# The first normalization's shift and scale in two halves of the channels, and the first projection begun on the lower half

## The chip, the core and the metric

The program runs on one NeuronCore of a Trainium2 chip. Its time is the device time of one execution in microseconds, given as the median of several runs. A NeuronCore has a matrix engine (TensorE, PE in the rows; PEld is its weight load), a vector engine (VectorE, DVE), an activation engine (ScalarE, ACT), a general engine (GpSimd, POOL), and a queue that mostly issues transfers (SyncE, SP). Each works through its own list of instructions in order and waits for the others by semaphores.

## What is computed

Two layers of a hybrid model over 512 tokens of 1024 channels. What matters here is the head of a layer:

```python
mod_all = einsum('bd,lde->lbe', silu(c), ada_w) + ada_b      # 6 vectors of 1024 a layer
sh1, sc1, g1, sh2, sc2, g2 = split(mod_all[l], 6)
h = _rms_norm(x, norm_mix_g[l]) * (1.0 + sc1) + sh1
proj = h @ w_in[l]                                           # 1024 -> 2732 columns
...
x = x + g1 * (mix @ w_out[l])
h2 = _rms_norm(x, norm_ffn_g[l]) * (1.0 + sc2) + sh2
x = x + g2 * _moe(h2, ...)
```

Four mixers (sparse attention, pooling, a linear recurrence, dilated attention) stand between `proj` and `mix`. All is in float32: each large product is made of three passes (`mm3`, L597) over a high part and a low part of both operands, so a weight tile is split into `wh` (a copy on ACT, L550) and `wl` (a difference on DVE, L551) before PE uses it.

## The kernel before

Tokens lie in four tiles of 128 (`xt`), channels in eight blocks of 128, called `k` = 0 to 7. Names that the text uses:

- **x**: four loads of 512 KB (L514). ACT squares and sums each tile in two halves (`square`, L788), DVE turns the four sums into `rs` (`rsqrt`), and ACT and DVE scale the tiles by it (L856 to L860).
- **tp**: four PE transposes for each block `k` (L868). ACT copies the result into `hf` (L876).
- **ada**: the product of silu(c) with `ada_w`. A unit of the stream `ada_s` is a 512 KB tile of two channel blocks by 512 output columns. The vectors scale (v = 1) and shift (v = 0) of the first normalization have two halves of 512 columns each (`jj`), and a half takes four units, so 16 units in all. Each unit is read by two program matmuls (L659), each of which leaves two records in the trace. DVE adds the partial sums to the table `MT` (L662). Four small matmuls `mc` (L721) turn the table into columns, from which DVE makes `A1` = (1 + scale) times gain (L882) and `B1` = shift (L883).
- **hH, hL**: block by block, `hf` becomes `hf * A1 + B1` (even blocks on DVE L897, odd ones on ACT L895), then its high part `hH` (ACT L898) and its low part `hL` (DVE L900).
- **c0**: the first 512 columns of the projection, transposed (`cchunk`, L908). Weights come in four units `u` of two channel blocks each; for each unit four sums `c` get six matmuls (L598 to L600), so 96 in all, 24 a unit. Block `k` = 2u + i of `hH` and `hL` is needed by unit `u` only. `c1` and others follow.

Loads are issued by the SP queue in the order in which the program asks for them (`Stream.load`, L563). The order on the other engines is written out by a planner (`_Weaver`, L366): a main stream of work is interleaved with side streams, by a clock of its own that adds up estimated durations (`_Clock`, L211). A side stream gets its next piece once that clock of PE has passed the moment at which the piece should be ready. So a change in the first stage also moves that clock, and by it the place of side work later on.

Of the kernel before, what the change touches and what calls it, by code (L numbers as in the profile page):

```python
# [11 lines left out]
F32 = mybir.dt.float32  # L12
# [4 lines left out]
AF = mybir.ActivationFunctionType  # L17
OP = mybir.AluOpType
# [416 lines left out]
def fused(ctx: ExitStack, tc: tile.TileContext, A, out, dbg=None):  # L435
    nc = tc.nc
    V, SC, PE, GP, SY = nc.vector, nc.scalar, nc.tensor, nc.gpsimd, nc.sync
# [12 lines left out]
    W = _Weaver(K)  # L450

    def G(name, shape=(1024,), dt=F32):

        t_ = gp.tile([128] + list(shape), dt, name=name, tag="g")
        K.alloc("g", NG, t_)
        return t_

    def HG(name, shape=(512,), dt=F32):

        t_ = hp.tile([128] + list(shape), dt, name=name, tag="h")  # L460
        K.alloc("h", NH, t_)
        return t_
# [4 lines left out]
    def TI(name, w=64, dt=F32):  # L467
        return tip.tile([128, w], dt, name=name, tag="ti")

    def PA(name):  # L470
        t_ = pa.tile([128, 512], F32, name=name, tag="a")
        K.alloc("a", NPA, t_)
        return t_

    def PB(name):
        t_ = pb.tile([128, 512], F32, name=name, tag="b")
        K.alloc("b", 8 - NPA, t_)
        return t_
# [31 lines left out]
    def load_x(src, q=None):  # L510
        r = []
        for t in range(NT):
            x_ = G("x")
            (q or SY).dma_start(x_, src[t * 128:(t + 1) * 128])  # L514
            r.append(x_)
        return r


    def rsqrt(x_, out_, n):

        xh, t_ = TI("rq_xh", n), TI("rq_t", n)
        V.tensor_scalar(xh, x_, -0.5, None, op0=OP.mult)
        V.tensor_scalar(out_.bitcast(I32), x_.bitcast(I32), 1, 0x7fffffff,
                        op0=OP.logical_shift_right, op1=OP.bitwise_xor)
        V.tensor_scalar(out_, out_, 1.835e-20, None, op0=OP.mult)
        for _ in range(3):
            V.tensor_tensor(t_, out_, out_, op=OP.mult)
            V.tensor_tensor(t_, t_, xh, op=OP.mult)
            V.scalar_tensor_tensor(out_, t_, 1.5, out_, op0=OP.add, op1=OP.mult)
# [67 lines left out]
    def mm3(o, sh, sl, mh, ml, first, last):  # L597
        PE.matmul(o, lhsT=sh, rhs=mh, start=first, stop=False)  # L598
        PE.matmul(o, lhsT=sh, rhs=ml, start=False, stop=False)  # L599
        PE.matmul(o, lhsT=sl, rhs=mh, start=False, stop=last)  # L600
# [23 lines left out]
    zc = cst.tile([128, 8, 63], F32, name="zc")  # L624
# [8 lines left out]
    MT = cst.tile([128, 512], F32, name="mt")  # L633
    MF = {(l, v): _Flag() for l in range(L) for v in range(6)}

    def mod_rows(l):
        GP.memset(MT, 0.0)
        GP.dma_start(MT[0:12], A["ada_b"][l])
        if l + 1 < L:
            GP.dma_start(MT[12:16], A["ada_b"][l + 1, 0:4])  # L640


    ada_s = Stream([(A["ada_w"][l, 2 * v + jj, u], 512) for l, v in
                    [(0, v) for v in (1, 0, 2, 4, 3, 5)] + [(1, v) for v in (1, 0, 2, 4, 3, 5)]
                    for jj in range(2) for u in range(4)], 3, raw=True)

    def ada(l, vs, more=True):
        if more:
            ada_s.cap += 8 * len(vs)
        for l2, v in vs:  # L650
            for jj in range(2):
                j = 12 * (l2 - l) + 2 * v + jj
                ps = PB("ada")
                for u2 in range(2):
                    raws = [ada_s.get() for _ in range(2)]
                    yield
                    for i in range(4):
                        g, k = 32 * i, 4 * u2 + i
                        PE.matmul(ps[g:g + 32], lhsT=zc[:, k, 31 - j:63 - j], rhs=raws[i // 2][:, i % 2],  # L659
                                  start=u2 == 0, stop=u2 == 1)  # L660
                    if u2:
                        V.tensor_tensor(MT, MT, ps, op=OP.add)  # L662
                    MF[l2, v].done, MF[l2, v].ready = u2 == jj == 1, K.mark
                    yield
# [52 lines left out]
    def mcol(p_, j0, n):  # L717

        v_ = p_[:, 0:4 * n].rearrange("p (q j) -> p q j", q=4)
        for q in range(4):  # L720
            PE.matmul(v_[:, q], lhsT=MT[:, q * 128:(q + 1) * 128], rhs=C("sel")[:, j0:j0 + n], start=True, stop=True)  # L721
        return v_

    def qj(ap):

        return ap.rearrange("p (j q) -> p q j", j=2)
# [61 lines left out]
    def square(x_, ms):  # L788

        m2 = TI("m2", 2)  # L790
        for j in range(2):
            SC.activation(PB("jk"), x_[:, j * 512:(j + 1) * 512], AF.Square, accum_out=m2[:, j:j + 1])
        V.tensor_tensor(ms, m2[:, 0:1], m2[:, 1:2], op=OP.add)

    def rms(xt, n=NT):
        ms = TI("ms", n)
        for t in range(n):
            square(xt[t], ms[:, t:t + 1])
        V.tensor_scalar(ms, ms, 1.0 / D, EPS, op0=OP.mult, op1=OP.add)
        rs_ = TI("rs_", n)  # L800
        rsqrt(ms, rs_, n)
        return rs_
# [38 lines left out]
    def layer(l, xt, mixs, moes, nmixs):  # L841
        last = l + 1 == L
        P_ = pars.pop(l)
        col, pr, omm, hv = P_.col, P_.pr, P_.omm, P_.hv
# [8 lines left out]
        if l == 0:  # L853
            P_.scaled()
            rs = rms(xt)
            for t in range(NT):  # L856
                if t % 2:
                    V.tensor_scalar(xt[t], xt[t], rs[:, t:t + 1], None, op0=OP.mult)
                else:
                    SC.activation(xt[t], xt[t], AF.Copy, scale=rs[:, t:t + 1])  # L860
        hH = [G("hH", (2, 512), F32R) for _ in range(4)]
        hL = [G("hL", (2, 512), F32R) for _ in range(4)]
        hf = [G("hf", (2, 512)) for _ in range(4)] if l == 0 else None

        def transposed(k):
            tp = PB("tp")
            for t in range(NT):
                PE.transpose(tp[:, t * 128:(t + 1) * 128], xt[t][:, k * 128:(k + 1) * 128], ident)  # L868
            return tp

        if l == 0:
            mc = PA("mc")
            A1, B1 = TI("A1", 8), TI("B1", 8)
            for k in range(8):
                tp = transposed(k)
                SC.activation(hf[k // 2][:, k % 2], tp, AF.Copy)  # L876
            ada_s.cap = 16
            ada_s.load(16)
            mixs.load(2)
            yield W.spawn(ada(0, [(0, 1), (0, 0)], False))  # L880
            mcv = mcol(mc, 0, 4)
            V.scalar_tensor_tensor(qj(A1), mcv[:, :, 2:4], 1.0, qj(col("gmix", 0, 8)), op0=OP.add, op1=OP.mult)  # L882
            V.tensor_copy(qj(B1), mcv[:, :, 0:2])  # L883
        else:
            A1, B1 = P_.A1, P_.B1
        parts = [(hH[k // 2][:, k % 2], hL[k // 2][:, k % 2]) for k in range(8)]
        late = None
        for k in range(8):
            if l == 0:
                src = f_ = hf[k // 2][:, k % 2]  # L890
            else:
                src = transposed(k)
                f_ = HG("hf1")
            if k % 2:
                SC.activation(f_, src, AF.Identity, scale=A1[:, k:k + 1], bias=B1[:, k:k + 1])  # L895
            else:
                V.tensor_scalar(f_, src, A1[:, k:k + 1], B1[:, k:k + 1], op0=OP.mult, op1=OP.add)  # L897
            SC.activation(parts[k][0], f_, AF.Copy)  # L898
            if late:
                V.tensor_tensor(late[2], late[0], late[1].bitcast(F32), op=OP.subtract)  # L900
            late = (f_,) + parts[k]
        V.tensor_tensor(late[2], late[0], late[1].bitcast(F32), op=OP.subtract)
        hH = [hH[k // 2][:, k % 2] for k in range(8)]
        hL = [hL[k // 2][:, k % 2] for k in range(8)]
        yield
# [2 lines left out]
        def cchunk(name, evac):  # L908
            n = len(CHUNKS[name])
            ps = [PA(name) for _ in range(n // 128)]  # L910
            for u in range(4):
                wh, wl = mixs.get()
                for c in range(n // 128):
                    cs_ = slice(c * 128, (c + 1) * 128)
                    for i in range(2):
                        k = 2 * u + i
                        mm3(ps[c], wh[:, i, cs_], wl[:, i, cs_], hH[k], hL[k], k == 0, k == 7)
                    if u == 3:
                        evac(c, ps[c])
                    yield  # L920
# [804 lines left out]
        for j in range(0, len(pairs), 6):  # L1725
            i = pairs[j][0]
# [21 lines left out]
        xt, XQ, HQ = RP.x, (SY, GP, SC)[XWQ], (SY, GP, SC)[HWQ]  # L1748
# [133 lines left out]
        late = []  # L1882
# [16 lines left out]
        for jj in range(2):  # L1899
# [23 lines left out]
            if jj == 0:  # L1923
                moes.load(LD[0])
                ps = [PA("wo") for _ in range(NT)]
# [9 lines left out]
            else:  # L1935
                us = [mixs.get() for _ in range(4)]
                rsides = []
                for t in range(NT):
                    ps = PA("wo")
# [276 lines left out]
        xt = load_x(xs_d)  # L2216
        rsn_, ms = TI("rsn_", 4), TI("ms", 4)
# [54 lines left out]
```

## Time and profile before

| | us |
|---|---|
| time, median of three runs | 1303.9 (1301.61 to 1309.27) |
| the profiled execution, own time | 1304.65 |
| span from its first to its last instruction | 1302.7 |
| PE busy | 1124.0 (86%) |
| DVE busy | 912.6 (70%) |
| ACT busy | 564.6 (43%) |
| first matmul of the projection starts at | 46.39 |

The profile is one execution with every instruction's start and end. "Busy" for PE is modelled, since matmuls are pipelined: their starts are a better guide than their lengths. The granted clock is TensorE's: 1.00 is 2.4 GHz and 0.50 is 1.2 GHz.

### The profile page before, as it was taken

How to read it: one execution, taken by the hardware profiler on the slowest of the kernel's cores; microseconds unless marked ns; L12 is line 12 of the kernel's file. 1: busy time of each engine (PE TensorE's matmuls, PEld its weight loads, DVE VectorE, ACT ScalarE, POOL GpSimd, SP SyncE). 2: the span in 40 equal slices, each digit the busy share in tenths (PEclk: the TensorE clock that was granted, in tenths of full speed). 3: DMA queues.
4: the chain of work that ended last, by engine and by line, in shares of the span. 5: the costliest groups of instructions: out<-in, count | busy, mean ns of one | idle time of the engine just before them, and what ended most of it. 6: DMA issues, size and time to landing. Idle time of an engine off the chain costs nothing. (4 is left out here: it accounts for less than half of the span.)

```text
span 1302.7 us, 21804 instructions
## 1 busy us (share of the span) xinstructions
PE 1124.0 (86%) x8166; PEld 866.9 (67%) x8166; DVE 912.6 (70%) x2300; ACT 564.6 (43%) x1052; POOL 175.7 (13%) x150
## 2 busy tenths in 40 slices
PE   4698999997999758999839989998979993899995
PEld 2485777656888646777728767784678882667774
DVE  2537566767664769999945396856676567899995
ACT  4443024333444226676635320344245431666662
POOL 2000000200000221233210000001000013123331
PEclk9798899998999969999979989999989996999998
DMA  9402000784523476999751111028430618599982
GB/s 351 184 33 82 33 29 29 277 295 163 197 100 111 159 285 230 347 338 353 277 177 46 49 66 50 21 96 300 158 111 29 211 52 335 204 314 342 353 304 36
DMA packets 68320, 232.05 MB, mean 178 GB/s; under 512 B 10580, under 2 KB 11460, under 8 KB 68208
## 3 DMA queue, kind: packets, MB, share of 16 engines
q1 hardware_dynamic: 54960, 192.18, 40.5%
q0 software_dynamic: 10368, 27.92, 7.8%
q10 hardware_dynamic: 2880, 10.49, 2.1%
q8 instruction: 67, 1.10, 0.3%
q14 instruction: 45, 0.37, 0.1%
HBM read 213.76 MB, written 25.17 MB: 183 GB/s over the span
## 5 line engine op out<-in xcount | busy, mean ns | idle before, releaser
L551 DVE TENSOR_TENSOR wl<-raw,wh 128x1024 fp32r<-128x1024 f32 (+2 forms) x256 | 301.6, 1194 | 39.5 <-ACT wh L550 36.4
L550 ACT ACTIVATE wh<-raw 128x1024 fp32r<-128x1024 f32 (+2 forms) x256 | 252.6, 1037 | 16.1 <-DMA raw<-w_out 6.2
L600 PE MATMUL gu<-wh,el 128*128 128x512 f32 x256 | 101.8, 398 | 3.4 <-DVE el L551 2.4
L598 PE MATMUL gu<-wh,eh 128*128 128x512 f32 x256 | 103.1, 403 | 0.6 <-ACT eh L550 0.6
L599 PE MATMUL gu<-wl,eh 128*128 128x512 f32 x256 | 99.8, 390 | 0.0
L598 PE MATMUL c<-hH,wh 128*128 128x512 f32 x176 | 72.1, 410 | 9.7 <-ACT wh L550 9.7
L598 PE MATMUL t<-wh,hH 128*128 128x512 f32 (+1 forms) x192 | 79.4, 414 | 0.0
L1587 PE MATMUL s<-kt,qt 128*128 128x128 f32 x480 | 67.1, 291 | 13.2 <-DVE mx L1590 13.2
L1593 ACT ACTIVATE P<-P,mx 128x128 f32<-128x128 f32 (+3 forms) x96 | 53.1, 554 | 56.2 <-DVE mx L1590 55.8
L599 PE MATMUL t<-wl,hH 128*128 128x512 f32 (+1 forms) x192 | 71.2, 371 | 5.7 <-DVE wl L551 5.7
L1587 PEld LDWEIGHTS s<-kt,qt 128*128 128x128 f32 x480 | 61.7, 203 | 18.6 <-DVE mx L1590 13.6
L600 PE MATMUL c<-hH,wl 128*128 128x512 f32 x176 | 70.5, 401 | 3.5 <-DVE wl L551 3.5
L600 PE MATMUL t<-wh,hL 128*128 128x512 f32 (+1 forms) x192 | 70.7, 368 | 0.0
L599 PE MATMUL c<-hL,wh 128*128 128x512 f32 x176 | 70.1, 398 | 0.0
L550 ACT ACTIVATE eh<-etp 128x512 fp32r<-128x512 f32 x64 | 34.8, 594 | 77.8 <-PE etp L2029 59.0
L598 PE MATMUL dp<-wh,ahl 128*128 128x512 f32 x128 | 53.5, 418 | 15.1 <-ACT ahl L550 15.1
L600 PE MATMUL dp<-wh,ahl 128*128 128x512 f32 x128 | 53.4, 417 | 12.8 <-DVE ahl L551 12.8
L1621 PEld LDWEIGHTS o<-vdt,pt 128*128 128x128 f32 x480 | 56.7, 192 | 8.3 <-DVE oa L1626 2.5
L600 PEld LDWEIGHTS gu<-wh,el 128*128 128x128 f32 x256 | 48.0, 188 | 19.0 <-DVE el L551 8.7
L1621 PE MATMUL o<-vdt,pt 128*128 128x64 f32 x480 | 59.9, 275 | 0.2
L659 PE MATMUL ada<-raw,zc 128*32 128x512 f32 x384 | 53.9, 622 | 0.6 <-DMA raw<-ada_w 0.5
L598 PEld LDWEIGHTS gu<-wh,eh 128*128 128x128 f32 x256 | 48.2, 188 | 9.3 <-ACT eh L550 1.0
(594 smaller groups left out, 2398.6 us busy)
## 6 DMA issues: line engine op xcount, KB each, us to landing
raw<-w_gu SPq DMA_DIRECT2D x120, 512.0 KB
raw<-ada_w SPq DMA_DIRECT2D x96, 512.0 KB
raw<-w_dn SPq DMA_DIRECT2D x60, 512.0 KB
raw<-win_c SPq DMA_DIRECT2D x16, 512.0 KB
raw<-win_t SPq DMA_DIRECT2D x16, 512.0 KB
raw<-w_out SPq DMA_DIRECT2D x16, 512.0 KB
x<-x SPq DMA_DIRECT2D x8, 512.0 KB
h2d<-h SPq DMA_DIRECT2D x8, 512.0 KB
```

The source lines that it names most:

```text
L550: SC.activation(h_, src, AF.Copy)
L551: eng.tensor_tensor(l_, src, h_.bitcast(F32), op=OP.subtract)
L598: PE.matmul(o, lhsT=sh, rhs=mh, start=first, stop=False)
L599: PE.matmul(o, lhsT=sh, rhs=ml, start=False, stop=False)
L600: PE.matmul(o, lhsT=sl, rhs=mh, start=False, stop=last)
L659: PE.matmul(ps[g:g + 32], lhsT=zc[:, k, 31 - j:63 - j], rhs=raws[i // 2][:, i % 2], start=u2 == 0, stop=u2 == 1)
L1587: PE.matmul(ss_[par][:, kb * 128:(kb + 1) * 128], lhsT=Q[i][0][:, hp], rhs=Q[kb][1][:, kj, par], start=True, stop=True)
L1593: SC.activation(P[:, par, :n], P[:, par, :n], AF.Exp, scale=-1.0, bias=mx[:, par:par + 1], accum_out=den[:, par:par + 1])
L1621: PE.matmul(o[:, par * 64:(par + 1) * 64], lhsT=pt[:, par, kb * 128:(kb + 1) * 128], rhs=vals, start=kb == 0, stop=kb == i)
```

## The change

The 16 units of `ada_w` are loaded in another order: first the eight that make the lower 512 channels of scale and shift, then the eight of the upper. `ada_first(jj)` makes the sums of one half in one PSUM tile and adds them to the table once. `mixs` (the projection's weights) has its first four units loaded between them. For the lower half the program goes through `raise_` (transposes and copies, now shared by ACT and DVE), `cols` (A1, B1 of four blocks) and `part_of` (the blocks' `hf`, `hH`, `hL`); then it begins `c0`. The upper half runs the same steps as a side stream `upper_half`, and `c0` asks for its end before the third unit (`u == 2`). In `rms`, tiles 1 and 3 are squared and summed by one DVE instruction instead of two on ACT.

```diff
--- before.py
+++ after.py
@@ -640,9 +640,24 @@
             GP.dma_start(MT[12:16], A["ada_b"][l + 1, 0:4])
 
 
-    ada_s = Stream([(A["ada_w"][l, 2 * v + jj, u], 512) for l, v in
-                    [(0, v) for v in (1, 0, 2, 4, 3, 5)] + [(1, v) for v in (1, 0, 2, 4, 3, 5)]
-                    for jj in range(2) for u in range(4)], 3, raw=True)
+    ada_s = Stream([(A["ada_w"][l, 2 * v + jj, u], 512) for l, v, jj in
+                    [(0, v, jj) for jj in range(2) for v in (1, 0)] +
+                    [(l, v, jj) for l, vs in ((0, (2, 4, 3, 5)), (1, (1, 0, 2, 4, 3, 5))) for v in vs for jj in range(2)]
+                    for u in range(4)], 3, raw=True)
+
+    def ada_first(jj):
+
+        ps = PB("ada")
+        for v in (1, 0):
+            j = 2 * v + jj
+            for u2 in range(2):
+                raws = [ada_s.get() for _ in range(2)]
+                for i in range(4):
+                    g, k = 32 * i, 4 * u2 + i
+                    PE.matmul(ps[g:g + 32], lhsT=zc[:, k, 31 - j:63 - j], rhs=raws[i // 2][:, i % 2],
+                              start=v == 1 and u2 == 0, stop=v == 0 and u2 == 1)
+                yield
+        V.tensor_tensor(MT, MT, ps, op=OP.add)
 
     def ada(l, vs, more=True):
         if more:
@@ -795,7 +810,11 @@
     def rms(xt, n=NT):
         ms = TI("ms", n)
         for t in range(n):
-            square(xt[t], ms[:, t:t + 1])
+            if t % 2:
+                V.tensor_tensor_reduce(G("jk"), xt[t], xt[t], 1.0, 0.0, op0=OP.mult, op1=OP.add,
+                                       accum_out=ms[:, t:t + 1])
+            else:
+                square(xt[t], ms[:, t:t + 1])
         V.tensor_scalar(ms, ms, 1.0 / D, EPS, op0=OP.mult, op1=OP.add)
         rs_ = TI("rs_", n)
         rsqrt(ms, rs_, n)
@@ -868,38 +887,74 @@
                 PE.transpose(tp[:, t * 128:(t + 1) * 128], xt[t][:, k * 128:(k + 1) * 128], ident)
             return tp
 
+        A1, B1 = (TI("A1", 8), TI("B1", 8)) if l == 0 else (P_.A1, P_.B1)
+        parts = [(hH[k // 2][:, k % 2], hL[k // 2][:, k % 2]) for k in range(8)]
+
+        def part_of(ks, late=None):
+
+            for k in ks:
+                if l == 0:
+                    src = f_ = hf[k // 2][:, k % 2]
+                else:
+                    src = transposed(k)
+                    f_ = HG("hf1")
+                if k % 2:
+                    SC.activation(f_, src, AF.Identity, scale=A1[:, k:k + 1], bias=B1[:, k:k + 1])
+                else:
+                    V.tensor_scalar(f_, src, A1[:, k:k + 1], B1[:, k:k + 1], op0=OP.mult, op1=OP.add)
+                SC.activation(parts[k][0], f_, AF.Copy)
+                if late:
+                    V.tensor_tensor(late[2], late[0], late[1].bitcast(F32), op=OP.subtract)
+                late = (f_,) + parts[k]
+                yield
+            V.tensor_tensor(late[2], late[0], late[1].bitcast(F32), op=OP.subtract)
+
+        upper = None
         if l == 0:
-            mc = PA("mc")
-            A1, B1 = TI("A1", 8), TI("B1", 8)
-            for k in range(8):
+            def raise_(k):
                 tp = transposed(k)
-                SC.activation(hf[k // 2][:, k % 2], tp, AF.Copy)
+                if k % 2:
+                    V.tensor_copy(hf[k // 2][:, k % 2], tp)
+                else:
+                    SC.activation(hf[k // 2][:, k % 2], tp, AF.Copy)
+
+            def cols(jj):
+                mcv = mcol(PB("mc"), 0, 4)
+                hs_ = slice(4 * jj, 4 * jj + 4)
+                V.scalar_tensor_tensor(A1[:, hs_], mcv[:, :, 2 + jj], 1.0, col("gmix", 4 * jj, 4), op0=OP.add, op1=OP.mult)
+                V.tensor_copy(B1[:, hs_], mcv[:, :, jj])
+
+            def upper_half():
+                for k in range(4, 8):
+                    raise_(k)
+                    yield
+                yield from ada_first(1)
+                cols(1)
+                yield
+                yield from part_of(range(4, 8))
+
             ada_s.cap = 16
+            ada_s.load(8)
+            mixs.load(2)
+            ada_s.load(12)
+            mixs.load(3)
             ada_s.load(16)
-            mixs.load(2)
-            yield W.spawn(ada(0, [(0, 1), (0, 0)], False))
-            mcv = mcol(mc, 0, 4)
-            V.scalar_tensor_tensor(qj(A1), mcv[:, :, 2:4], 1.0, qj(col("gmix", 0, 8)), op0=OP.add, op1=OP.mult)
-            V.tensor_copy(qj(B1), mcv[:, :, 0:2])
+            mixs.load(4)
+            steps = ada_first(0)
+            for _ in range(3):
+                next(steps)
+            for k in range(4):
+                raise_(k)
+            for _ in steps:
+                pass
+            cols(0)
+            for i, _ in enumerate(part_of(range(4))):
+                if i == 1:
+                    mixs.presplit(1)
+            upper = W.spawn(upper_half(), front=True)
         else:
-            A1, B1 = P_.A1, P_.B1
-        parts = [(hH[k // 2][:, k % 2], hL[k // 2][:, k % 2]) for k in range(8)]
-        late = None
-        for k in range(8):
-            if l == 0:
-                src = f_ = hf[k // 2][:, k % 2]
-            else:
-                src = transposed(k)
-                f_ = HG("hf1")
-            if k % 2:
-                SC.activation(f_, src, AF.Identity, scale=A1[:, k:k + 1], bias=B1[:, k:k + 1])
-            else:
-                V.tensor_scalar(f_, src, A1[:, k:k + 1], B1[:, k:k + 1], op0=OP.mult, op1=OP.add)
-            SC.activation(parts[k][0], f_, AF.Copy)
-            if late:
-                V.tensor_tensor(late[2], late[0], late[1].bitcast(F32), op=OP.subtract)
-            late = (f_,) + parts[k]
-        V.tensor_tensor(late[2], late[0], late[1].bitcast(F32), op=OP.subtract)
+            for _ in part_of(range(8)):
+                pass
         hH = [hH[k // 2][:, k % 2] for k in range(8)]
         hL = [hL[k // 2][:, k % 2] for k in range(8)]
         yield
@@ -910,6 +965,8 @@
             ps = [PA(name) for _ in range(n // 128)]
             for u in range(4):
                 wh, wl = mixs.get()
+                if u == 2 and upper is not None:
+                    yield upper
                 for c in range(n // 128):
                     cs_ = slice(c * 128, (c + 1) * 128)
                     for i in range(2):
```

**SP at the start, before** (x, then the ada units, then the projection's units):

```order
L514 DMA x<-x 128x1024 x4
L567 DMA raw<-ada_w 128x1024 x16
L567 DMA raw<-win_c 128x1024 x8
L567 DMA raw<-win_c 128x768 x4
```

**and after**, up to the same place:

```order
L514 DMA x<-x 128x1024 x4
L567 DMA raw<-ada_w 128x1024 x8
L567 DMA raw<-win_c 128x1024 x2
L567 DMA raw<-ada_w 128x1024 x4
L567 DMA raw<-win_c 128x1024
L567 DMA raw<-ada_w 128x1024 x4
L567 DMA raw<-win_c 128x1024 x5
L567 DMA raw<-win_c 128x768 x4
```

Two units of the projection now stand ahead of the upper eight ada units, and one in their middle; the number of transfers is the same.

**PE at the start, before** (`tp` transposes, `ada` products, `mc` columns, `c_366` the first sum of c0):

```order
L868 MATMUL tp<-cbase,x 128x128 x32
L659 MATMUL ada<-raw,zc 32x512 x32
L721 MATMUL mc<-cbase,mt 128x4 x4
L598 MATMUL c_366<-hH,wh 128x512
L599 MATMUL c_366<-hL,wh 128x512
L600 MATMUL c_366<-hH,wl 128x512
```

**and after** (line numbers are those of the changed file; `c_308` and `c_309` are sums of c0):

```order
L657 MATMUL ada<-raw,zc 32x512 x12
L887 MATMUL tp<-cbase,x 128x128 x16
L657 MATMUL ada<-raw,zc 32x512 x4
L736 MATMUL mc<-cbase,mt 128x4 x4
L598 MATMUL c_308<-hH,wh 128x512
L599 MATMUL c_308<-hL,wh 128x512
L600 MATMUL c_308<-hH,wl 128x512
L598 MATMUL c_308<-hH,wh 128x512
L599 MATMUL c_308<-hL,wh 128x512
L600 MATMUL c_308<-hH,wl 128x512
L887 MATMUL tp<-cbase,x 128x128 x4
```

Twelve ada products stand ahead of the first transposes, only half of the transposes ahead of c0, and the others between its matmuls.

**PE at the end of c0's second unit, after:**

```order
L887 MATMUL tp<-cbase,x 128x128 x4
L598 MATMUL c_311<-hH,wh 128x512
L599 MATMUL c_311<-hL,wh 128x512
L600 MATMUL c_311<-hH,wl 128x512
L598 MATMUL c_311<-hH,wh 128x512
L599 MATMUL c_311<-hL,wh 128x512
L600 MATMUL c_311<-hH,wl 128x512
L657 MATMUL ada<-raw,zc 32x512 x16
L736 MATMUL mc<-cbase,mt 128x4 x4
L598 MATMUL c_308<-hH,wh 128x512
L599 MATMUL c_308<-hL,wh 128x512
L600 MATMUL c_308<-hH,wl 128x512
```

All 16 products of the upper half, and its `mc`, stand behind the 48 matmuls of units 0 and 1 and ahead of unit 2.

**PE in the second layer, where the third part of the projection ends, before** (`cps` is the compression of keys for sparse attention, `mp` the first products of the recurrence's inverse, `t` a projection sum, `bs` the recurrence's bonus):

```order
L598 MATMUL t_7465<-wh,hH 128x512
L599 MATMUL t_7465<-wl,hH 128x512
L600 MATMUL t_7465<-wh,hL 128x512
L1424 MATMUL cps<-kv,w_7493 64x33 x32
L1424 MATMUL cps<-kv,w_7527 64x33 x32
L598 MATMUL t_7466<-wh,hH 128x512
L599 MATMUL t_7466<-wl,hH 128x512
L600 MATMUL t_7466<-wh,hL 128x512
L598 MATMUL t_7466<-wh,hH 128x512
L599 MATMUL t_7466<-wl,hH 128x512
L600 MATMUL t_7466<-wh,hL 128x512
L1092 MATMUL mp<-ar,bk 128x128 x8
```

**and after:**

```order
L598 MATMUL t_7460<-wh,hH 128x512
L599 MATMUL t_7460<-wl,hH 128x512
L600 MATMUL t_7460<-wh,hL 128x512
L1149 MATMUL mp<-ar,bk 128x128 x8
L598 MATMUL t_7461<-wh,hH 128x512
L599 MATMUL t_7461<-wl,hH 128x512
L600 MATMUL t_7461<-wh,hL 128x512
L598 MATMUL t_7461<-wh,hH 128x512
L599 MATMUL t_7461<-wl,hH 128x512
L600 MATMUL t_7461<-wh,hL 128x512
L1125 MATMUL bs<-la,c_rwkv 128x512
L1149 MATMUL mp<-ar,bk 128x128 x4
```

The second layer's code is the same, but the planner's clock now puts `mp` ahead of `cps`. Similar shifts stand at three other places: one in the first layer's inverse, and two in the second layer, in the rest of the inverse and in the last third of attention. Elsewhere the order on all engines is the same as before, up to swaps of neighbours.

## Rows read from the trace of the kernel before

**Rows 1.** The page, busy time of engines and the costliest group of DVE.

```profile
PE 1124.0 (86%) x8166; PEld 866.9 (67%) x8166; DVE 912.6 (70%) x2300; ACT 564.6 (43%) x1052; POOL 175.7 (13%) x150
...
L551 DVE TENSOR_TENSOR wl<-raw,wh 128x1024 fp32r<-128x1024 f32 (+2 forms) x256 | 301.6, 1194 | 39.5 <-ACT wh L550 36.4
```

**Rows 2.** The first 30 us: PE, PEld, DVE, ACT, POOL busy; clock, DMA, GB/s.

```profile
0.00:30.00 30.00, 11.96 (x80) 7.63 (x80) 8.19 (x47) 13.36 (x28) 8.26 (x19) 1.00 0.95 346
```

**Rows 3.** The same view in stretches of 2 us, where the granted clock falls and rises.

```profile
38.00:40.00 2.00, 0.00 (x0) 0.00 (x0) 1.43 (x3) 1.97 (x4) 0.00 (x0) 0.50 0.99 393
...
52.00:54.00 2.00, 2.00 (x10) 1.64 (x9) 0.86 (x5) 1.19 (x3) 0.00 (x0) 1.00 0.00 0
```

**Rows 4.** Timeline (start us, us, engine, line, operands): transposes and the ada weight loads.

```profile
18.72 6.04 PE L868 MATMUL tp<-cbase,x 128*128 128x128 f32 x30 [0.35 <-ACT x L860]
...
25.14 0.13 PEld L659 LDWEIGHTS ada<-raw,zc 128*32 128x32 f32 x4 [0.30 <-issue]
25.57 0.13 PEld L659 LDWEIGHTS ada<-raw,zc 128*32 128x32 f32 x4 [0.30 <-issue]
...
32.53 0.14 PEld L659 LDWEIGHTS ada<-raw,zc 128*32 128x32 f32 x4 [1.13 <-DMA raw<-ada_w]
33.82 0.14 PEld L659 LDWEIGHTS ada<-raw,zc 128*32 128x32 f32 x4 [1.15 <-DMA raw<-ada_w]
```

**Rows 5.** Timeline: from the sum of the ada products to the first projection.

```profile
34.93 0.69 DVE L662 TENSOR_TENSOR mt<-mt,ada 128x512 f32<-128x512 f32 x1 [4.12 <-PE ada L659]
...
37.69 0.63 ACT L898 ACTIVATE hH<-hf 128x512 fp32r<-128x512 f32 x1 [12.25 <-DVE hf L897]
38.23 0.80 ACT L895 ACTIVATE hf<-hf,B,A 128x512 f32<-128x512 f32 x1
38.35 0.69 DVE L900 TENSOR_TENSOR hL<-hf,hH 128x512 fp32r<-128x512 f32 x1 [0.69 <-ACT hH L898]
...
39.06 1.15 ACT L898 ACTIVATE hH<-hf 128x512 fp32r<-128x512 f32 x2
...
45.30 1.99 ACT L550 ACTIVATE wh<-raw 128x1024 fp32r<-128x1024 f32 x2
...
46.39 0.79 PE L598 MATMUL c<-hH,wh 128*128 128x512 f32 x1 [9.67 <-ACT wh L550]
...
47.65 0.80 PE L600 MATMUL c<-hH,wl 128*128 128x512 f32 x1
```

**Rows 6.** Timeline of PE in the first projection, at half and at full clock.

```profile
48.24 0.63 PE L598 MATMUL c<-hH,wh 128*128 128x512 f32 x1
...
48.67 0.63 PE L599 MATMUL c<-hL,wh 128*128 128x512 f32 x1
...
52.41 0.40 PE L598 MATMUL c<-hH,wh 128*128 128x512 f32 x1
...
70.10 0.39 PE L598 MATMUL c<-hH,wh 128*128 128x512 f32 x1
```

**Rows 7.** Timeline of ACT: it reads the first projection's last sum.

```profile
70.98 0.69 ACT L939 ACTIVATE zk<-c,omm 128x512 f32<-128x512 f32 x1 [0.67 <-PE c L600]
```

**Rows 8.** DVE's fused multiply and reduction elsewhere (ns min/median/max).

```profile
L1590 DVE CUSTOM_DVE_ANT_0 P<-s,c_attn x96: 283/488/693, 266.8 to 1016.5; 128x128 f32<-128x128 f32 x24, 128x512 f32<-128x512 f32 x24, 128x256 f32<-128x256 f32 x24, 128x384 f32<-128x384 f32 x24
```

**Rows 9.** PE's waits of the second layer, from 740 to 860 us.

```profile
PE c L600 <- DVE wl L551: 3.5, 1, 3.5
```

**Rows 10.** Stretches of 4 us around that wait.

```profile
760.00:764.00 4.00, 3.55 (x7) 1.38 (x8) 3.93 (x9) 0.70 (x2) 0.00 (x0) 0.66 0.51 179
764.00:768.00 4.00, 4.00 (x10) 3.13 (x11) 3.97 (x9) 1.19 (x2) 0.00 (x0) 0.50 0.02 7
```

**Rows 11.** PE's waits of the second layer, from 930 to 1010 us.

```profile
PE s L1587 <- DVE mx L1590: 7.0, 1, 7.0
```

**Rows 12.** Stretches around it.

```profile
950.00:955.00 5.00, 3.31 (x14) 3.20 (x15) 4.35 (x14) 3.19 (x8) 0.00 (x0) 0.50 0.02 3
...
970.00:980.00 10.00, 9.99 (x90) 9.68 (x89) 5.35 (x24) 3.90 (x14) 0.00 (x0) 1.00 0.86 300
```

## The prediction

> **What bounds the kernel now.** I first read the page: PE is busy for 86% of the span, and the costliest group of DVE is the split of weights, with 1.19 us for a tile [rows 1]. Then I looked at the start by stretches. In its first 30 us DMA is at 0.95 and PE works for 12 us [rows 2]: the loads bound this stage. After the last load comes a chain through DVE, PE and ACT, in which PE stands still and its clock is granted at 0.50 [rows 3]; from 52.41 us to the end of the first projection c0 PE issues matmuls without a gap, 78 of them in 17.69 us, 0.227 us each [rows 6]. So from there on PE itself is the limit, and a microsecond won or lost at c0's end moves what follows by about as much. ACT reads c0's last sum at 70.98 [rows 7]; I call 70.9 us c0's end. The question is only when c0 ends in the changed kernel, and what the planner's new order does later.
>
> **The loads.** The last two ada units arrive 1.29 us apart, at 32.53 and 33.82 [rows 4]. Counted back in such steps from unit 16, unit 6 is there at 20.9 and unit 8 at 23.5. These come in the same place of the queue as before. The eight upper units now have three units of the projection ahead of them, so the last is there at 33.82 + 3 x 1.29 = 37.7 us instead of 33.8.
>
> **The squares.** Two of four tiles go from ACT to one DVE instruction. DVE's reductions of this form take 283 ns for 128 columns and 693 for 512 [rows 8], so some 1.07 ns a column, and 1.24 us for 1024 as an estimate; ACT needs about as much for two halves. The last tile's sum is the one that counts, and its load sets its start. I take no gain; bounds are 0.3 us either way.
>
> **The lower half.** PE's list has 12 ada products (units 1 to 6), 16 transposes, and then units 7 and 8. An ada unit takes 0.43 us (25.14 to 25.57) and 30 transposes went from 18.72 to 24.69, 0.20 us each [rows 4]. So: unit 6 at 20.9, its product done at 21.35, transposes done at 24.55, unit 8's product begins at 25.0. From there I copy the chain of before. The sum on DVE starts 1.11 us after the last product began (33.82 to 34.93), the first hH 2.76 us after that (37.69) [rows 4, 5]: hH0 starts at 28.9. The next ones on ACT are the odd block (0.54 later), its hH (1.37 later), and then, about 0.6 later, the split of the first weight unit, at 30.9. PE's first matmul stood 1.09 us behind that split (45.30 to 46.39) [rows 5]: **c0 begins at 32.0 instead of 46.4**. That is the gain that the change aims at, 14.4 us.
>
> **What it is worth.** Only 48 of c0's 96 matmuls can use it. They need the low half of the weights (1.26 us behind the first matmul [rows 5]) and the second block's hL, which now stands on DVE behind that split; I place it at 34.5, with five matmuls done. The other 43 take 43 x 0.227 = 9.8 us, and the remaining 16 transposes, which now stand between them, 3.2: together 12.9 at full clock. But PE stood still before, so the clock will be low, as it was in c0 before: 0.43 us a matmul at 48.24, full speed by 52.41 [rows 6]. That cost about 2.4 us (4.8 us at half speed), and I add the same here: 34.5 + 12.9 + 2.4 = 49.8 us.
>
> **The upper half.** Its loads have long landed by then (37.7). But all 16 products stand on PE behind those 48 matmuls, and nothing behind them can run ahead. They take 8 x 0.43 = 3.4 us, so the last begins at 52.8. The bare chain follows a second time: sum at 53.9, hH4 at 56.7, its hL 0.66 later for 0.69 us, hH5 1.37 us behind hH4 and 0.6 long, hL5 done 0.7 later at 59.4 [rows 5]. Four matmuls slip in between; 44 are left. They need 44 x 0.227 = 10.0 us, so 69.4 at full clock. PE has again been without steady work, from 53.2 to 59.4, longer than where its clock was at 0.50 before (38 us, after products that ended at 35 [rows 3, 4]). So I add 2.4 us again: **c0 ends at 71.8 us, 0.9 us later than before**. DVE's and ACT's other new work in between (copies of four transposes, the rope tables, two weight splits of 1.19 us [rows 1]) fits, in my placing, ahead of the upper sum with less than 1 us to spare; a miss costs up to one split.
>
> The bounds of the sum: with no loss of clock at all it ends at 71.8 - 4.8 = 67.0, which is 3.9 us less than now; with a second stall of clock of the same size or the late split, at 74.2, 3.3 us more.
>
> The clock is where a rule speaks against the change. The trace shows 0.50 in the break before c0 and 1.00 after some microseconds of dense matmuls [rows 3, 6]. The Trainium skill ("TensorE: Matmul & The Clock Gate", Part 1: The HAM clock gate) says that the low clock is the default state and that activity releases it, so a kernel that opens a second break pays the restart a second time. By that rule the end is at 71.8; if the earlier, sparser work of PE kept the clock up, it is at 67.0. The rows agree with the rule for the one break that is there.
>
> **The rest of the program.** The order of the first layer is the same but for one block of the recurrence's inverse between projection matmuls, where I take nothing. In the second layer the planner puts the inverse ahead of the compression, and orders the last third of attention anew. No work is added. The trace of before shows what such places can cost: PE's wait of 3.5 us for a weight split, with the clock at 0.66 and 0.50 in the 8 us around it [rows 9, 10], and one of 7.0 us for attention's maximum, with 0.50 behind it [rows 11, 12]. I take zero, between a gain of the first and a loss like the second.
>
> **The sum.** 1304.65 us is the profiled execution's own time, 0.75 above the median of 1303.9. With +0.9 us it is 1305.5, against the median 1304.8: **no change that can be measured**. Half a percent, 6.5 us, is about what a measurement of this kernel can tell from no change.
>
> **Rivals.**
>
> *The clock stays up.* PE has some work all along from about 15 us on (the ada products no longer wait for the transposes), and the four transposes between groups of matmuls fill gaps. Against it: before, three products of 0.43 us in 4 us were followed by a fall [rows 3, 4], and here 28 to 32 us is as empty. c0's end moves by -3.9 us: 1300.0. Still within half a percent.
>
> *A new wait in the second layer's attention.* There PE works 9.99 of 10 us at full clock from 970 to 980 [rows 12], and this stretch is ordered anew. If a score matmul there comes to stand ahead of the maximum that frees its place, as at the wait of 7.0 us [rows 11], PE stands for 7.0 us and then works at half clock for 3.3 us [rows 12], 1.65 lost: 8.65 + 0.9 on top of 1303.9 gives 1313.5, slower. It decides from the point where DVE's list of maxima and copies is later than PE's list by more than one group. For it: the planner goes by estimates; against it: nothing waits there now, and DVE is busy only 5.35 of those 10 us.
>
> *The second layer loses a wait.* With the inverse's first products in the place of the compression, DVE gets to its splits in another order. If the wait of 3.5 us goes and the clock stays up around it (4 x 0.34 + 4 x 0.50 = 3.4 us [rows 9, 10]), this is 6.9 us: 1297.9, and with a little help from the clock at the start it is more than half a percent faster.
>
> That the change doesn't do what it says I leave out: the order of instructions shows units 0 and 1 of c0 ahead of the upper half's products.
>
> **How the numbers follow.** My forecast, c0's end within 2.5 us of now and nothing later, has 0.54 (1301 to 1308). The clock that stays up has 0.16, the new wait 0.17, the lost wait 0.13. Faster by over half a percent is some two thirds of the last and a little of the second: 0.11. Slower is the new wait and the forecast's late end together with a small one: 0.19. The same: 0.70. The range leaves out most of the new wait and the far side of the lost one: 1297.5 to 1311.
>
> **What would show it.** In the changed kernel's trace: the first matmul of c0 near 32 us; the last ada product near 53 with PE idle behind it until about 57; two stretches of half clock, near 32 to 39 and 58 to 64; c0's last sum read near 72. It would be wrong if the upper products run much before 50 us, if the clock is at 1.00 throughout 30 to 65, or if the second layer is longer or shorter than before by more than 5 us from its first projection to its expert stage.

## The result, and the profile after

The changed kernel takes 1315.25 us at the median, the kernel before beside it 1304.84: a ratio of 1.0084 (95% interval 1.0059 to 1.0109). I had said 1304.8 us and no change; it is 0.84% slower, and outside the range. The profiled execution took 1315.25 us for a span of 1313.4, at a mean granted clock of 0.939 (before: 0.943).

The page, PE's busy time and the weight splits on DVE, as in [rows 1]:

```profile
PE 1136.7 (87%) x8174; PEld 869.9 (66%) x8174; DVE 917.3 (70%) x2306; ACT 559.5 (43%) x1040; POOL 175.1 (13%) x150
...
L551 DVE TENSOR_TENSOR wl<-raw,wh 128x1024 fp32r<-128x1024 f32 (+2 forms) x256 | 301.8, 1195 | 46.7 <-ACT wh L550 41.5
```

The split is the same, and PE has 12.7 us more of busy time with as good as the same products. By an estimate about half of that is half clock: weighted by the granted clock of its trace, PE's busy time loses 41.6 us to it, before 34.2. The start, by the timelines of PE, DVE and ACT (the places of [rows 4 to 7]):

```profile
21.53 2.00 PE L887 MATMUL tp<-cbase,x 128*128 128x128 f32 x16
...
30.40 0.79 PE L598 MATMUL c<-hH,wh 128*128 128x512 f32 x1 [3.95 <-ACT wh L550]
33.73 1.05 PE L887 MATMUL tp<-cbase,x 128*128 128x128 f32 x4
39.21 0.60 PE L887 MATMUL tp<-cbase,x 128*128 128x128 f32 x4
45.69 3.64 PE L657 MATMUL ada<-raw,zc 128*32 128x512 f32 x32
...
49.42 0.69 DVE L660 TENSOR_TENSOR mt<-mt,ada 128x512 f32<-128x512 f32 x1 [0.19 <-PE ada L657]
...
52.10 0.63 ACT L905 ACTIVATE hH<-hf 128x512 fp32r<-128x512 f32 x1 [4.12 <-DVE hf L904]
...
52.78 0.79 PE L598 MATMUL c<-hH,wh 128*128 128x512 f32 x1 [1.56 <-ACT hH L905]
...
66.89 0.69 ACT L996 ACTIVATE zk<-c,omm 128x512 f32<-128x512 f32 x1 [0.67 <-PE c L600]
```

c0 begins at 30.40 for 46.39, stands still again behind the 16 upper products, and its last sum is read at 66.89 for 70.98 [rows 7]: the edited stage **wins 4.1 us**. Stretches of 4 us there (columns as in [rows 2]) show the clock fall twice, where [rows 3] had one fall:

```profile
28.00:32.00 4.00, 1.56 (x3) 0.84 (x4) 2.32 (x4) 2.31 (x4) 0.00 (x0) 0.50 1.03 411
32.00:36.00 4.00, 4.00 (x14) 2.85 (x14) 2.97 (x5) 3.86 (x6) 0.00 (x0) 0.67 1.02 405
...
52.00:56.00 4.00, 3.21 (x7) 2.00 (x8) 2.51 (x5) 3.83 (x7) 0.00 (x0) 0.50 0.01 4
56.00:60.00 4.00, 4.00 (x14) 3.17 (x13) 1.92 (x2) 0.94 (x1) 0.00 (x0) 0.68 0.28 98
60.00:64.00 4.00, 4.00 (x20) 3.29 (x19) 0.47 (x1) 0.69 (x1) 0.00 (x0) 1.00 0.00 0
```

So the loss lies later. This table holds the starts of the same instructions in the traces (us; in brackets, against before). `mvp` is a product behind layer 1's inverses, `wo` the projection behind attention, `c` and `t` layer 2's two projections, `dp` the experts' second product. "Old order" is the first experiment below.

| | before | changed | changed, layer 2 in old order |
|---|---|---|---|
| last `zk`, end of c0 | 71.0 | 66.9 (-4.1) | 67.8 (-3.2) |
| first `mvp`, layer 1 | 220.6 | 213.1 (-7.5) | 214.2 (-6.4) |
| last `wo`, layer 1 | 447.2 | 441.1 (-6.1) | 439.0 (-8.2) |
| last `c`, layer 2 | 768.4 | 762.1 (-6.3) | 760.1 (-8.3) |
| last `t`, layer 2 | 882.5 | 883.0 (+0.5) | 874.2 (-8.3) |
| last `wo`, layer 2 | 1076.6 | 1084.6 (+8.0) | 1068.2 (-8.4) |
| last `dp`, layer 2 | 1290.3 | 1300.5 (+10.2) | 1284.2 (-6.1) |

The changed kernel is 6 us ahead until layer 2's `t`; there it loses 6.8 us, in layer 2's attention 7.5, and 2.2 in the last stage. Those first two are the places where the planner put the same work in another order. A difference of 2 us between two traces can come from the execution alone: up to layer 1's last `wo` the changed kernel and the one with layer 2 in the old order have the same order, and they stand at 441.1 and 439.0.

In layer 2's projections PE's waits from 755 to 880 us now have this row (`tps` and `xps` are products of the recurrence's inverse, `tz` what DVE makes of the one for the other), and DVE and PE run so around it:

```profile
PE xps L1187 <- DVE tz L1183: 2.1, 2, 1.8
```

```profile
784.38 0.71 DVE L1142 STREAM_TRANSPOSE X<-Y 128x512 f32<-128x512 f32 x1
785.02 0.65 DVE L1393 TENSOR_TENSOR ps<-pu 128x511 f32<-128x511 f32 x1
...
789.81 0.22 DVE L1494 COPY gv<-ge 64x128 f32<-64x128 f32 x1
790.07 0.42 DVE L1183 TENSOR_TENSOR tz<-tps,c_rwkv 128x256 f32<-128x256 f32 x1
...
786.08 1.12 PE L1181 MATMUL tps<-X,lm 64*64 64x32 f32 x32
788.39 0.39 PE L600 MATMUL t<-wh,hL 128*128 128x512 f32 x1
790.55 1.12 PE L1187 MATMUL xps<-tz,Y 64*64 64x32 f32 x32 [1.76 <-DVE tz L1183]
```

PE's `tps` is done at 787.2, but DVE works through 17 instructions of the pooling and compression side first (785.02 to 790.03), and only then takes `tz`, for which the inverse's next product waits. In stretches of 5 us, what this starts:

```profile
785.00:790.00 5.00, 3.78 (x43) 2.64 (x42) 4.39 (x18) 0.89 (x2) 0.00 (x0) 1.00 0.07 26
790.00:795.00 5.00, 4.45 (x62) 3.53 (x62) 2.70 (x5) 1.23 (x2) 0.00 (x0) 0.74 0.00 0
795.00:800.00 5.00, 5.00 (x53) 3.86 (x52) 0.43 (x2) 0.00 (x0) 0.00 (x0) 0.58 0.01 3
```

The wait itself is 1.76 us; then the clock is at half for a while, and (0.26 + 0.42) x 5 = 3.4 us more go to that, together 5.2 of the 6.8. The wait that stood in [rows 9] is still there (3.5 us, between 750 and 755).

In layer 2's attention, PE's waits from 930 to 1030 us, for the single wait of [rows 11]:

```profile
PE s L1644 <- DVE mx L1647: 10.1, 4, 7.0
...
PE ctp L1623 <- DVE scm L1618: 0.5, 1, 0.5
```

The score products `s` wait three times more for the maxima `mx`, 3.1 us in all. From 930 us to the last `s`, before and after:

```profile
930.00:1015.90 85.90, 78.57 (x640) 69.88 (x638) 60.14 (x214) 40.18 (x114) 0.56 (x1) 0.94 0.21 70
```

```profile
930.00:1024.50 94.50, 82.36 (x656) 71.95 (x655) 61.32 (x216) 40.28 (x114) 0.56 (x1) 0.95 0.23 74
```

PE works 82.36 of 94.5 us; before it was 78.57 of 85.9. That is 4.8 us more without work, and 3.8 more of busy time. The clock has no part in it (0.95, before 0.94); 18 more `o` products of attention now stand ahead of the last `s`, and what else makes up the 3.8 us stays open.

### The profile page after: what moved, and what is told of

Same layout as the page of the kernel before. It is cut to its first block, busy times and chain, and to the rows that moved or that the text cites. A ratio compares the mean times of both kernels' runs of the same rounds, so it can differ in the third digit from the quotient of the medians.

```text
span 1313.4 us, 21790 instructions
## 1 busy us (share of the span) xinstructions
PE 1136.7 (87%) x8174; PEld 869.9 (66%) x8174; DVE 917.3 (70%) x2306; ACT 559.5 (43%) x1040; POOL 175.1 (13%) x150
## 5 line engine op out<-in xcount | busy, mean ns | idle before, releaser
L599 PE MATMUL t<-wl,hH 128*128 128x512 f32 (+1 forms) x192 | 71.5, 372 | 5.7 <-DVE wl L551 5.7
L598 PE MATMUL dp<-wh,ahl 128*128 128x512 f32 x128 | 53.6, 418 | 15.1 <-ACT ahl L550 15.1
L599 PEld LDWEIGHTS gu<-wl,eh 128*128 128x128 f32 x256 | 48.6, 190 | 10.5 <-DVE wl L551 1.4
```

## The experiments

In all of these the steps that the planner `_Weaver` chose were written out, for the phases named, as a list of the generators to step (a dot is one step of the main chain), so that only the order differs:

```diff
     def run(self, main):
-        for r in main:
+        main = iter(main)
+        while True:
+            t = self.order.pop(0) if self.order else "."
+            if t != ".":
+                s = [s for s in self._able() if s.n == t][0]
+                self._step(s)
+                continue
...
```

All ratios are against the kernel before, beside it on the same chip. What each changes against which kernel:

| run | median us | ratio (95% interval) |
|---|---|---|
| e1_old2: changed, layer 2 in the order before | 1300.21 | 0.9976 (0.9964 to 0.9989) |
| e2_oldproj2: only its projections | 1305.93 | 1.0029 (1.0011 to 1.0047) |
| e3_oldatt2: only its attention | 1306.92 | 1.0033 (1.0014 to 1.0053) |
| e4_new2: before, layer 2 in the new order | 1321.0 | 1.0138 (1.0123 to 1.0152) |
| e5_oldall: changed, order before from c0's end on | 1302.76 | 0.9979 (0.9967 to 0.9991) |
| e6_upper_early: as e1, upper products earlier | 1304.11 | 0.9982 (0.9957 to 1.0008) |
| e8_pool_back: as e3, pooling and compression back | 1301.69 | 0.9982 (0.9971 to 0.9994) |
| e7_act_squares: as e1, all squares on ACT again | 1299.24 | one execution |

**Is it the order of layer 2?** Four kernels, in which either part of it is old or new.

> The changed kernel, with the order of its work in layer 2 (projections and attention) written out as the kernel before has it, so that layer 1 alone is new. Theory A (the planner's new order in layer 2 costs the time; the edit itself gains): the 6.2 us that the trace of the changed kernel is ahead at the end of layer 1 stay, 1304.8 - 6.2 = 1298.6 us, between 1297 and 1301, faster than both. Rival B (layer 2 is slowed by something other than its order: its weights' transfers, the clock's phase after an earlier start): the time stays near the changed kernel's 1315 us.

> The changed kernel with the order before in layer 2's projections alone; layer 2's attention keeps its new order. Theory A: the 6.7 us lost in the projections come back, the 7.4 us lost in the attention and the 2.3 us at its end stay: 1298.6 + 9.7 = 1308.3 us (1305 to 1310). If the attention's loss only follows from the projections' (one late tile carried on), it goes too: 1298.6 us. Rival B: 1315.

> The changed kernel with the order before in layer 2's attention alone; layer 2's projections keep their new order. Theory A: 1298.6 + 6.7 = 1305.3 us, 1304 to 1308 (above if the 2.3 us at the attention's end come from the projections). Rival B: 1315.

> The kernel before with the new order in layer 2's projections and attention and nothing else. Theory A: it loses what the changed kernel lost there, 6.7 + 7.4 + 2.3 = 16.4 us on 1304.8: 1321 us (1318 to 1323). Rival B (the loss needs the edited first stage): 1305.

It is. With the old order the changed kernel is 0.24% under the kernel before; with the new order alone the kernel before loses 18 us (four executions). The parts add up: from e1 to e3 the new projections cost 0.57% (7.4 us), from e1 to e2 the new attention 0.53% (6.9 us), together 14.3, and the changed kernel stands 1.08% (14.1 us) over e1. That the order costs 18 us in the kernel before and 14 in the changed one lies within the intervals. Each loss needs its own order only: from the last `c` to the last `t` the traces with the new projections take 120.8 to 120.9 us, those with the old 114.1 to 114.6, and e2 and e4 have the four waits for the maxima (10.1 us) where e1 has the one of 7.0. Which step of attention's new order brings these waits no run isolates. Rival B falls. The 2.2 us at the end are not the order's: e1's trace loses them too (table above, -8.4 to -6.1), and over all traces this stretch takes 213.6 to 215.9 us, with either order. The edit's own worth is 3 us by e1 and 7 us between e4 and the changed kernel (1.0138 to 1.0084); the one trace had shown 6 at layer 1's end.

**Which move in the projections?** Only the pooling and compression step goes back ahead of the inverses; their other new places stay:

```diff
-. inverse3 inverse2 . rwkv1 bonus2 bonus2 inverse3 . ... . inverse2 pool1 compress1 . inverse3
+. pool1 compress1 inverse3 inverse2 . rwkv1 bonus2 bonus2 inverse3 . ... . inverse2 . inverse3
```

> The changed kernel with the order before in layer 2's attention, and in its projections the new order but for one move: the step of the pooling and compression side (64 + 64 cps matmuls and 16 short DVE instructions, 5.3 us of DVE) stands ahead of the inverses again. Theory A (the 1.8 us that PE waits for tz behind that block of DVE work, and the half clock that follows, are the loss): the 6.7 us between e3_oldatt2 and e1_old2 come back, 1300 us. Rival (the inverses' and bonus steps' new places cost the time): 1305 to 1307 us, as e3_oldatt2.

PE's waits from 755 to 885 us in it:

```profile
PE c L626 <- DVE wl L577: 3.5, 1, 3.5
PE xps L1213 <- DVE tz L1209: 1.2, 2, 0.8
```

The long wait for `tz` is gone (0.8 us is the longest left) and no stretch from 765 to 805 is below a clock of 1.00. Of the 0.57% it brings back 0.51%. At its place the trace shows less: from the last `c` to the last `t` it takes 116.6 us, for 120.9 in the changed kernel and 114.1 in e1, so 4.3 of 6.8 us are back. There are still 1.2 us of waits for `tz`, and 1.2 for `qn` where e1 has 0.5. So the block of DVE work between `tps` and `tz` is the larger part of the cause, as A says; the rest lies in other new places of the same order.

**Did the swapped inverse block in layer 1 help?** My traces of the changed kernel and of e1 win another 3 us between c0's end and `mvp`.

> The changed first stage alone: from the end of c0 on, both layers have the order of the kernel before, so the block of layer 1's inverses that the planner swapped is undone too. The last zk should end near 67.8 us as in e1_old2, 3.2 to 4.1 us earlier than before. Theory A (the swapped inverse block is worth nothing, as the prediction took it): the same as e1_old2, 1300 us. Rival (the 3.4 to 4 us that the traces of the changed kernel and of e1_old2 win between the first cps and the first mvp come from the swap): 1303 us, no gain over the kernel before but 0 to 1 us.

With the old order, PE's waits from 140 to 222 us and two stretches:

```profile
PE xps L1217 <- DVE tz L1213: 2.3, 2, 1.9
```

```profile
145.00:150.00 5.00, 3.11 (x41) 2.36 (x40) 3.22 (x14) 2.12 (x3) 0.00 (x0) 0.95 0.01 3
150.00:155.00 5.00, 5.00 (x40) 3.81 (x39) 1.49 (x2) 0.00 (x0) 0.00 (x0) 0.50 0.00 0
```

And e1, with the swap, in the same views:

```profile
PE qt L1483 <- DVE qn L827: 2.4, 2, 1.2
```

```profile
150.00:155.00 5.00, 5.00 (x77) 4.05 (x76) 2.93 (x5) 0.00 (x0) 0.00 (x0) 1.00 0.00 0
```

At its place the swap does in layer 1 what the compression's move undoes in layer 2: it takes the 1.9 us wait for `tz` away, and the low clock behind it. But the totals are 0.9979 and 0.9976: not to be told apart. The median of 1302.76 us stands at the rival's 1303, the ratio at A's: neither is settled. (e7 below has the swap, and paid 3.5 us for low clock at 180 to 190 us instead.)

**Can the second break at c0 be closed?** In PE's order the upper products go from behind the second weight unit to behind the first step of it (u is a step of the upper half; the steps of the rope tables stand behind them now):

```diff
-. u . u . rope . u . . . u rope . . u u rope u u u u u u u u
+. u . u . u . u . u u u u u . u . u . u . u u rope rope rope
```

> As e1_old2, but the 16 products of the upper channel half stand in PE's order right after the first weight unit of c0 (behind its first step of the second) in place of behind the second, so that the transposes, shift, scale and splits of the upper half are worked out beside the second unit's matmuls. Theory A (the upper weights have landed by then; what the changed kernel loses at 49.4 to 58.4 us is 3.4 us of waiting and some 3 us of half clock): the last zk ends 5 to 6.5 us earlier than in e1_old2, near 62 us, and the time is 1294 to 1296 us. Rival (the upper weights land later than 39 us, so PE waits for them where it worked before): the zk ends where e1_old2 has it or later, 1300 to 1303 us.

PE in it, and the two stretches behind the break (in the changed kernel 0.50 and 0.68):

```profile
41.56 3.64 PE L687 MATMUL ada<-raw,zc 128*32 128x512 f32 x32
46.01 1.05 PE L766 MATMUL mc<-cbase,mt 128*128 128x4 f32 x8 [0.81 <-DVE mt L690]
46.93 0.48 PE L628 MATMUL c<-hH,wh 128*128 128x512 f32 x1
```

```profile
48.00:52.00 4.00, 4.00 (x19) 3.32 (x18) 2.39 (x4) 3.97 (x6) 1.02 (x2) 1.00 0.00 0
52.00:56.00 4.00, 4.00 (x19) 3.31 (x18) 3.51 (x12) 2.23 (x4) 0.07 (x1) 1.00 0.54 150
```

The break shrinks to 0.8 us, the clock stays up, and the last `zk` starts at 62.2 us, 5.6 before e1: A, at its place. The total, for which A had 1294 to 1296 us, is not: its twelve times lie from 1295.8 to 1308.6 us, with a granted clock of 0.947 down to 0.936.

**Where does that go?** The same kernel was traced twice more.

> The kernel of e6_upper_early again, for a second trace: its twelve times stood in two groups, six from 1295.8 to 1303.4 us at a mean granted clock of 0.941 to 0.947 and six from 1304.8 to 1308.6 us at 0.936 to 0.941. Theory A (the groups differ in the time that TensorE spends at its low clock, nothing else): if this trace is of the long group, it shows more stretches at 0.50 than the first trace, at half of their length lost each, and between them the same pace; a time near 1307 us has some 8 to 10 us more lost to them. Rival (a transfer or another engine is late in the long group): the same stretches at 0.50, and a new wait.

> The same kernel a third time, for the same purpose and with the same expectations: two of three traces are likely to show both groups.

They took 1306.09 and 1302.45 us, the first trace 1298.33. Over the first 1290 us of each trace I summed (1 - clock) x 5 for the stretches of 5 us with a clock under 0.97: 68.0 us in the first, 71.5 in the one of 1302.45, 74.7 in the one of 1306.09. So the low clock accounts for 6.7 of the 7.8 us between the two ends. PE stands about as long in all three (span less busy time: 170.2, 170.1 and 169.2 us), so no new wait makes the difference. One stretch that only the trace of 1306.09 has, 360 to 370, lost 3.4 us; PE waits for nothing from 340 to 375. PE there (`rbp` are 16 small products), and the first 5 us of it:

```profile
359.55 2.40 PE L1779 MATMUL rbp<-cm__3491,b2c 128*128 128x16 f32 x16
```

```profile
360.00:365.00 5.00, 5.00 (x25) 4.48 (x25) 1.39 (x4) 1.39 (x4) 0.00 (x0) 0.57 0.00 0
```

And the first trace, at the same instructions:

```profile
355.43 1.85 PE L1779 MATMUL rbp<-cm__3491,b2c 128*128 128x16 f32 x16
```

```profile
355.00:360.00 5.00, 4.79 (x32) 3.68 (x32) 1.51 (x5) 2.16 (x8) 0.00 (x0) 1.00 0.02 3
```

A holds, then. Why some executions of one program have more of these stretches than others isn't settled.

**The squares.** In one execution two of the sums of squares go back to ACT:

```diff
-            if t % 2:
-                V.tensor_tensor_reduce(G("jk"), xt[t], xt[t], ...)
-            else:
-                square(xt[t], ms[:, t:t + 1])
+            square(xt[t], ms[:, t:t + 1])
```

> As e1_old2, but all four sums of squares of the first norm are taken by ACT again, as in the kernel before. Theory A (they stand on the path to the transposes): the scaling of x starts 0.8 us later, the first hH and the first c0 matmul too, 31.2 us for 30.4. Rival (the path goes through the lower weights and products): c0 begins at 30.4 as before.

c0 began at 31.12, as A says, but not for A's reason:

```profile
21.27 1.05 PE L687 MATMUL ada<-raw,zc 128*32 128x512 f32 x4 [0.22 <-DMA raw<-ada_w]
22.25 2.00 PE L913 MATMUL tp<-cbase,x 128*128 128x128 f32 x16
```

The transposes follow a product that waited for its weights, which landed 0.73 us later than in the changed kernel (20.54 there); `x` was scaled by 18.5, long before. ACT's first square, too, began 0.5 us later (8.61 for 8.11). The squares were not what held c0 up; whether they moved the loads, one execution doesn't tell.

## Why the prediction was wrong, by its own steps

**The lower half: right, but for the transposes.** I had c0 beginning at 32.0; it was 30.40. 16 transposes took 2.00 us where I put 3.2. I had 0.20 us each from 30 transposes in 6.04 us [rows 4]. Nothing paced that row: `x` was scaled by 18.7 us. The transposes themselves were slow there, all but the last few; first before (19.3 to 23.6 us and 24.1 to 24.7), then changed (ns min/median/max):

```profile
L868 PE MATMUL tp<-cbase,x x22: 421/421/421, 19.0 to 23.5; 128*128 128x128 f32 x22
L868 PE MATMUL tp<-cbase,x x7: 272/273/421, 23.7 to 24.5; 128*128 128x128 f32 x7
```

```profile
L887 PE MATMUL tp<-cbase,x x16: 272/273/328, 21.5 to 23.3; 128*128 128x128 f32 x16
```

They start 0.21 us apart until 23.9 us and 0.11 from there, as at half and full clock. That this was the clock is read from the spacing: the trace of before has no record of it until 23.97 us, and the view gives 1.00 for a stretch without one.

**What it is worth: two terms too large.** By 34.4 us six matmuls were done (I had five by 34.5). From there I had 49.8 for the start of the upper products, and it was 45.69. Two terms make up these 4.1 us: 12 transposes between the matmuls delayed them by 0.35 us for each four, 1.1 us for my 3.2 (for 16), and the clock was up from about 34.6 (0.67 in the stretch from 32 to 36), so that of the 2.4 us there some 0.7 were left. From c0's first matmul on the half clock lasted 4.2 us (30.40 to 34.6), and before 4.9 (46.39 to 51.3), and that was under the six matmuls that stood on their operands anyway; I had added the whole of it behind them.

**The upper half: right.** From the upper sum to hH4 2.68 us (I had 2.8), from there to c0's end 14.8 (15.1), with the second break and half clock from 52 to 58 us. The rule that I weighed there (the Trainium skill, "TensorE: Matmul & The Clock Gate", Part 1: The HAM clock gate), that a second break pays the restart a second time, agrees with the trace: 0.50 and 0.68 behind the break, and 1.00 from 36 us to c0's end when e6 closed it. c0's end moved by -4.1 us for my +0.9, and by -3.2 in e1 and -4.0 in e5. That is as much as my rival in which the clock stays up (-3.9), but the clock did not stay up: it is the two terms, and the agreement is luck.

**"I take nothing" for layer 1's inverse block: wrong at its place, unmeasurable in the total**, as e5 shows.

**"I take zero" for layer 2's order: the step that failed.** It cost 14 us. I let a gain and a loss of unlike size stand on either side of zero, though the order was known: what would have told was in the order itself. DVE's block of compression had come to stand between `tps` and `tz`, and that block has its durations in the trace of before. My rival of a new wait in attention was right in kind: score products behind the maxima that free their places. But it was three waits of 3.1 us in all for my one of 7.0, with no more half clock than before, and the 6.9 us, for my 8.65, are in part other time without work and busy time (above). I gave it 0.17, on the ground that DVE was busy only 5.35 of 10 us there; that is a mean, and doesn't say what is at the head of the queue. For the projections I had only a rival in which a wait goes; the 3.5 us wait stayed, and another came. Two of the three signs that I had named for being wrong came true: the upper products began at 45.69 us, and the second layer, from its last `c` to its last `dp`, is 16.5 us longer.

## What to carry to other kernels

When an edit makes a planner's clock run differently, its new order far behind the edit is part of the change and is priced like it, place by place: what stands on a consumer's queue between a PE product and the instruction that its next product needs. Holding the old order there is worth trying first; here that alone turns 0.84% slower into 0.24% faster. And a duration is taken from a row at the clock that the work will have: the transposes took 0.42 us each in one part of a row and 0.27 in the other.

## What the runs showed of the hardware

A PE wait of under 2 us can be followed by a half-clock stretch that costs more than the wait: 1.76 us, then 3.4 (785 to 800 us); in e5 1.9, then 3.4 (145 to 160 us: 0.95, 0.50 and 0.87). With the first of these waits (changed kernel, e3, e4) the clock falls at that place in all three traces, without it (e1, e2, e5 to e10) in none. Not every short wait does this: behind 1.2 us for `qn` in layer 1, at 180 us, the clock fell in e7 (0.69 and 0.62) and stayed at 1.00 in e1. The clock also fell while PE was busy for 5.00 of 5 us by the view, and not in each execution: 0.57 from 360 to 365 us, where `rbp`'s products of 16 columns run, at a place where the same program ran at 1.00 in another trace. The Trainium skill (the same page and section) says that the chip's watch of PE's activity runs free of the kernel's start, and that the restart varies from run to run. With the second these traces agree; the first no run here shows. The low clock is the larger part of the difference between two traces of e6, 6.7 of 7.8 us; its twelve times spread by 12.8 us.
